# Keys, queries and rotary queries: high weights against both halves of the latent in one 512-column product

## The chip, the cores and the metric

The kernel runs on one core of a Trainium2 chip. The metric is the device time of one execution, in microseconds; beside it stands the span of one profiled execution, from its first to its last instruction. Lower is better.

## The reference

One layer of an encoder over 256 tokens of width 2048, with a last RMSNorm. All arrays are float32. Only the latent attention is touched here:

```python
def mla_branch(q_lat, kv_lat, k_rope, cos, sin, q_norm_w, w_uq, kv_norm_w, w_ukv, w_o_attn):
    q = (rms_norm(q_lat, q_norm_w) @ w_uq).reshape(bsz, s_len, MLA_HEADS, QK_NOPE_DIM + QK_ROPE_DIM)
    q_nope, q_rope = q[..., :QK_NOPE_DIM], q[..., QK_NOPE_DIM:]
    q_rope = apply_rope(q_rope, cos[:, :, None, :], sin[:, :, None, :])
    kv = (rms_norm(kv_lat, kv_norm_w) @ w_ukv).reshape(bsz, s_len, MLA_HEADS, QK_NOPE_DIM + V_HEAD_DIM)
    k_nope, v = kv[..., :QK_NOPE_DIM], kv[..., QK_NOPE_DIM:]
    ...
        sc = (jnp.einsum("bqhd,bkhd->bhqk", qn, k_nope)
              + jnp.einsum("bqhr,bkr->bhqk", qr, k_rope))
        p = jax.nn.softmax(sc.astype(jnp.float32) * scale, axis=-1).astype(v.dtype)
        return jnp.einsum("bhqk,bkhd->bqhd", p, v)
```

Both latents have 512 channels; there are 16 heads of 128 plain and 64 rotary channels. Around it the layer has a combined input projection, a two-way SSD scan, an output projection and a gated feed-forward part, which make up most of the time.

## The kernel before, in words

Every large product is done in float32r, a format that TensorE takes at one pass, with each operand split in a high part and a low part: high x high, high x low and low x high are summed, low x low is dropped. Weights come as blocks of 128 x 128. A **job** is up to 16 blocks of weights that SyncE loads into one `raw` buffer (three of them); a job has two **halves** of eight blocks. For each half ScalarE (ACT) casts the high part (`wh`, line 151), and VectorE (DVE) subtracts it from the raw weights to get the low part (`wl`, line 152). There are five buffers each of `wh` and `wl` (`HB=5`), so the split runs up to five halves ahead of TensorE (PE).

Activations are held channels first, 128 channels x 256 tokens. The large projections (`dense`, lines 178 and 185) keep high and low activations side by side, so that one product of 512 columns multiplies a high weight block with both; a bank of PSUM then holds two sums of 256 columns, and the low weights add 256 columns to the first. `halves_sum` (lines 237 and 238) adds the two sums: an ACT copy of one, a DVE add of the other. Gate units (`quad`, lines 213 to 215) and `v_job` (lines 573 to 575) have the activations as the stationary operand, and hold two banks.

The latent attention uses another form, `mm3` (lines 157 to 159): three products of 256 columns for each block, high weight x high latent, high weight x low latent, low weight x high latent, all into one sum. `lat_norm2` (lines 424 and 425) splits a latent into `latH` and `latL`. `qk_job` i has in its first half the queries of two heads, and in its second their keys; a half is two blocks of 128 channels x four blocks of 128 latent channels, and its two results lie side by side in one bank `g`. ACT casts it to the high part of `qk` (line 596), DVE subtracts to get the low part (line 597). `r_job` does the rotary queries of eight heads in the same way, with one ACT copy of the bank (line 537), after which four DMAs on ACT's queue fetch the swapped halves (line 377).

PSUM has eight banks: four for `g` and four for `s`, the attention's own small products. In the attention stage the jobs stand as written in a list, where g is a unit of a gate quad (four units in a row fill the same two banks), R the rotary queries, V the values and QK queries with keys:

```python
"g R0 g g g V0 QK0 g QK1 V1 QK2 g QK3 V2 R1 g QK4 g QK5 V3 QK6 g QK7 g g g g g"
```

The attention of a head (`att1`, scores and exponentials; `att2`, transposes of the probabilities; `att3`, the product with the values) is hung onto the jobs that follow. A scheduler then orders each engine's instructions and hands out buffers and banks as they come free, so the order on an engine is not that of the lines. ACT and DVE work in that order, one instruction after the other, and so does PE.

Of the kernel before, what the change touches and what calls it, by code (L numbers as in the profile page):

```python
# [15 lines left out]
P = 128  # L16
S = 256
# [42 lines left out]
def tile_bidir_hybrid_layer(ctx: ExitStack, tc, xT, pos, vec, cst, w_in, w_r, w_v, w_qk, w_oa,  # L60
# [23 lines left out]
    def f32(ap):  # L84
        return ap.bitcast(F32)
# [330 lines left out]
    def lat_norm2(which, wname):  # L416
        ps = spread(lat[which + "v"])
        r = p1(name="r_" + which)
        act.activation(r, ps, AF.Copy)
        t = lat[which]  # L420
        for k in range(4):
            dve.scalar_tensor_tensor(t[:, k, :], t[:, k, :], vcol(wname, k), r, ALU.mult, ALU.mult)
        hi, lo = page([P, 4, S], F32R, name="latH"), page([P, 4, S], F32R, name="latL")
        act.activation(hi, t, AF.Copy)
        dve.tensor_sub(lo, t, f32(hi))
        lat[which + "HL"] = (hi, lo)


    dts = {}
# [93 lines left out]
            dve.tensor_sub(z[r], t[r, 0, :], f32(kr["h"][r]))  # L523

    def r_job(i):
        hi, lo = lat["qHL"]
        cell = {}

        def mm(h, n, wh, wl):
            ps = gpsum([P, 2, S])  # L530
            cell[h] = ps
            for b in range(2):
                for k in range(4):
                    mm3(ps[:, b, :], wh[:, 4 * b + k, :], wl[:, 4 * b + k, :], hi[:, k, :], lo[:, k, :],
                        k == 0, k == 3)
            t = page([P, 2, S], name="rf")
            act.activation(t, ps, AF.Copy)
            cell["f", h] = (t, swapped(t, 2))

        def ev():  # L540
            pass

        def ro():
            for h in range(2):
                q, sw = cell["f", h]
                rotate(q, sw, 2)


                t = page([P, 2, 2, S], F32R, name="rp")
                for j in range(2):  # L550
                    s0, s1 = slice(64 * j, 64 * j + 64), slice(64 - 64 * j, 128 - 64 * j)
                    act.activation(t[s0, j], q[s0], AF.Copy)
                    dve.tensor_sub(t[s1, j], q[s0], f32(t[s0, j]))
                rp[2 * i + h] = t
        j = Job(w_r[i], 16, mm, ev)
        jobs.append(j)
        return j, ro

    def v_job(i):
        hi, lo = lat["kvHL"]  # L560
        cell = {}

        def mm(h, n, wh, wl):
# [4 lines left out]
            for t in range(2):  # L568
                ts = slice(t * P, (t + 1) * P)
                for kk in range(2):  # L570
                    k = 2 * h + kk
                    ps = cell["ps"][t]
                    pe.matmul(ps, lhsT=hi[:, k, ts], rhs=wH[:, kk, :], start=k == 0, stop=False)
                    pe.matmul(ps, lhsT=hi[:, k, ts], rhs=wL[:, kk, :], start=False, stop=False)
                    pe.matmul(ps, lhsT=lo[:, k, ts], rhs=wH[:, kk, :], start=False, stop=k == 3)

        def ev():
            vh, vl = page([P, 2, 512], F32R, name="vh"), page([P, 2, 512], F32R, name="vl")
# [7 lines left out]

    def qk_job(i):
        def mm(h, n, wh, wl):
            hi, lo = lat["qHL" if h == 0 else "kvHL"]
            ps = gpsum([P, 2, S])  # L590
            for b in range(2):
                for k in range(4):
                    mm3(ps[:, b, :], wh[:, 4 * b + k, :], wl[:, 4 * b + k, :], hi[:, k, :], lo[:, k, :],
                        k == 0, k == 3)
            t = page([P, 2, 2, S], F32R, name="qk")
            act.activation(t[:, 0], ps, AF.Copy)
            dve.tensor_sub(t[:, 1], ps, f32(t[:, 0]))
            qk[i, h] = t
        j = Job(w_qk[i], 16, mm, lambda: None)
        jobs.append(j)  # L600
        return j
# [700 lines left out]
```

## Time and profile before

| | before |
|---|---|
| time, median of 3 runs | 1962.59 us (1961.36 to 1962.71) |
| profiled execution | 1962.68 us |
| its span | 1960.9 us |
| mean granted clock of TensorE | 0.998 |
| attention stage (first R job's products to last QK job's) | about 75 to 235 us |
| HBM read | 371.91 MB |

PE is the row of the matmuls, PEld that of the weight loads that lie under them. A matmul's row is longer than the distance to the next one's start, since matmuls are pipelined; so prices are taken from starts. A line can be that of a helper: `mm3`'s lines 157 to 159 serve other stages too, told apart by the tile names (`latH`, `latL`).

### The profile page before, as it was taken

The page shows a single profiled execution, that of the slowest core. Times are in us where ns is not written, and L with a number is a line of the kernel's source. Part 1 is how long each engine was busy: PE and PEld are TensorE (multiplying, and loading weights), DVE is VectorE, ACT ScalarE, POOL GpSimd, SP SyncE. Part 2 cuts the span into 40 slices and gives each one's busy share as a digit, 9 for nine tenths or more (in the row PEclk, how much of TensorE's full clock was granted, in tenths as well). Part 3 has the DMA queues.
Part 4 walks back from the last instruction along what each step waited for, and adds up shares of the span by engine and source line. Part 5 has one row for each costly group of instructions (what it writes and reads, how often), then busy time and mean ns, then how long its engine had stood idle before and what let it go on. Part 6 is the DMA issues. An engine that isn't in the chain of part 4 may idle for free.

```text
span 1960.9 us, 28920 instructions
## 1 busy us (share of the span) xinstructions
PE 1945.8 (99%) x11136; PEld 1707.2 (87%) x11136; DVE 1444.6 (74%) x2349; ACT 1205.3 (61%) x1878; POOL 0.2 (0%) x4
## 2 busy tenths in 40 slices
PE   9999999999999999999999999999999999999997
PEld 8889988888888888888888888888888888888887
DVE  7897744779779789879755566777656777557775
ACT  6566544687887887978644455666435655346553
POOL 0000000000000000000000000000000000000000
PEclk9999999999999999999999999999999999999999
DMA  7554456765665565565666665555555555555543
GB/s 279 179 173 154 137 172 216 251 222 172 215 233 173 198 234 194 194 215 182 205 196 198 200 222 176 190 193 192 181 189 190 194 192 175 194 192 193 188 161 124
DMA packets 93259, 379.31 MB, mean 193 GB/s; under 512 B 10688, under 2 KB 11328, under 8 KB 62912
## 3 DMA queue, kind: packets, MB, share of 16 engines
q1 hardware_dynamic: 91440, 375.09, 56.6%
q10 hardware_dynamic: 1680, 2.37, 0.4%
q8 instruction: 87, 1.43, 0.3%
q14 instruction: 52, 0.43, 0.1%
HBM read 371.91 MB, written 4.33 MB: 192 GB/s over the span
## 4 chain that ended last, share of the span: by engine, by line
PE 95%; DVE 3%; DMA 1%; ACT 1%; issue 0%; ACTq 0%; DVEq 0%; SPq 0%
PE g L178 42%; PE g L185 22%; PE g L214 7%; PE g L213 7%; PE g L215 7%; PE g L159 1%; PE g L157 1%; PE g L158 1%; DVE wl L152 1%; PE s L789 1%; PE s L798 1%; PE s L158 0%; PE s L159 0%; PE s L157 0%; PE s L771 0%; PE s L634 0%
## 5 line engine op out<-in xcount | busy, mean ns | idle before, releaser
L152 DVE TENSOR_TENSOR wl<-raw,wh 128x1024 fp32r<-128x1024 f32 (+1 forms) x670 | 802.7, 1209 | 328.1 <-ACT wh L151 181.3
L151 ACT ACTIVATE wh<-raw 128x1024 fp32r<-128x1024 f32 (+1 forms) x670 | 698.9, 1047 | 546.6 <-PE g L178 352.0
L178 PE MATMUL g<-xHL,wh 128*128 128x512 f32 x1424 | 341.7, 392 | 1.3 <-DVE xHL L291 1.1
L178 PE MATMUL g<-hHL,wh 128*128 128x512 f32 x1360 | 324.8, 391 | 0.0
L178 PEld LDWEIGHTS g<-xHL,wh 128*128 128x128 f32 x1424 | 262.4, 188 | 53.6 <-DVE xHL L291 1.5
L178 PEld LDWEIGHTS g<-hHL,wh 128*128 128x128 f32 x1360 | 249.8, 188 | 48.3
L185 PEld LDWEIGHTS g<-xHL,wl 128*128 128x128 f32 x1424 | 182.6, 191 | 7.0
L185 PE MATMUL g<-xHL,wl 128*128 128x256 f32 x1424 | 184.9, 283 | 0.0
L185 PEld LDWEIGHTS g<-hHL,wl 128*128 128x128 f32 x1360 | 174.3, 191 | 6.6
L185 PE MATMUL g<-hHL,wl 128*128 128x256 f32 x1360 | 176.4, 283 | 0.0
L178 PE MATMUL g<-aHL,wh 128*128 128x512 f32 x692 | 166.6, 391 | 0.1
L910 DVE SCALAR_TENSOR_TENSOR uc<-u,V,uc 128x255 f32<-128x255 f32 x176 | 85.3, 485 | 88.4 <-ACT uc L908 85.3
L178 PEld LDWEIGHTS g<-aHL,wh 128*128 128x128 f32 x692 | 126.9, 188 | 25.6 <-DVE aHL L928 1.3
L213 PE MATMUL g<-wh,yHL 128*128 128x512 f32 x256 | 100.1, 391 | 0.0
L214 PE MATMUL g<-wl,xHL 128*128 128x512 f32 x256 | 100.0, 391 | 0.0
L213 PE MATMUL g<-wh,xHL 128*128 128x512 f32 x256 | 100.0, 391 | 0.0
L215 PE MATMUL g<-wh,yHL 128*128 128x512 f32 x256 | 99.7, 389 | 0.0
L215 PE MATMUL g<-wh,xHL 128*128 128x512 f32 x256 | 99.6, 389 | 0.0
L214 PE MATMUL g<-wl,yHL 128*128 128x512 f32 x256 | 99.6, 389 | 0.0
L185 PEld LDWEIGHTS g<-aHL,wl 128*128 128x128 f32 x692 | 89.2, 191 | 3.6
L185 PE MATMUL g<-aHL,wl 128*128 128x256 f32 x692 | 90.4, 283 | 0.0
L684 DVE SCALAR_TENSOR_TENSOR xs<-cu,V,xs 128x254 f32<-128x254 f32 (+1 forms) x128 | 59.0, 479 | 0.2
(298 smaller groups left out, 2534.1 us busy)
## 6 DMA issues: line engine op xcount, KB each, us to landing
raw<-in_w_in SPq DMA_DIRECT2D x88, 1024.0 KB, 4.9
raw<-in_w_up SPq DMA_DIRECT2D x88, 1024.0 KB, 4.8
raw<-in_w_in SPq DMA_DIRECT2D x128, 256.0 KB, 3.9
raw<-in_w_os SPq DMA_DIRECT2D x128, 256.0 KB, 3.6
raw<-in_w_dn SPq DMA_DIRECT2D x32, 1024.0 KB, 5.0
raw<-in_w_oa SPq DMA_DIRECT2D x64, 256.0 KB, 3.9
FB<-acsD SPq DMA_DIRECT2D x32, 512.0 KB, 7.4
raw<-in_w_out SPq DMA_DIRECT2D x14, 1024.0 KB, 5.0
```

The costliest lines, as they stand in the source:

```text
L151: act.activation(vh, r, AF.Copy)
L152: dve.tensor_sub(vl, r, f32(vh))
L157: pe.matmul(ps, lhsT=wH, rhs=xH, start=first, stop=False)
L158: pe.matmul(ps, lhsT=wH, rhs=xL, start=False, stop=False)
L159: pe.matmul(ps, lhsT=wL, rhs=xH, start=False, stop=last)
L178: pe.matmul(ps, lhsT=wh[:, b, :], rhs=x, start=k == 0, stop=False)
L185: pe.matmul(cell["ps"][:, 0, :], lhsT=wl[:, b, :], rhs=get(k)[:, 0, :], start=False, stop=k == ktot - 1)
L213: pe.matmul(ps, lhsT=x[:, 0, ts], rhs=wH[:, kk, :], start=k == 0, stop=False)
L214: pe.matmul(ps, lhsT=x[:, 0, ts], rhs=wL[:, kk, :], start=False, stop=False)
L215: pe.matmul(ps, lhsT=x[:, 1, ts], rhs=wH[:, kk, :], start=False, stop=k == kt - 1)
L684: dve.scalar_tensor_tensor(o[:, a], u[:, b], vcol("cw", k * 48 + cb), o[:, a], ALU.mult, ALU.add)
L910: dve.scalar_tensor_tensor(o[:, a], u[:, b], vcol("fcw", k * 88 + cb), o[:, a], ALU.mult, ALU.add)
```

## The change

`lat_norm2` now lays high and low latent side by side (`latHL`, in two tiles of two channel blocks), and `two_blocks` replaces `mm3` in `r_job` and `qk_job`. A half takes two banks, one for each block of output channels: eight products of 512 columns with the high weights, four per bank; then eight of 256 columns with the low weights; then `halves_sum` on each bank into a page of SBUF (`qkf`, or `rf` itself). For `qk_job` the cast and the subtraction follow, now from that page and no longer from PSUM. `v_job` only reads the latents from the new tiles.

```diff
--- before.py
+++ after.py
@@ -420,10 +420,28 @@
         t = lat[which]
         for k in range(4):
             dve.scalar_tensor_tensor(t[:, k, :], t[:, k, :], vcol(wname, k), r, ALU.mult, ALU.mult)
-        hi, lo = page([P, 4, S], F32R, name="latH"), page([P, 4, S], F32R, name="latL")
-        act.activation(hi, t, AF.Copy)
-        dve.tensor_sub(lo, t, f32(hi))
-        lat[which + "HL"] = (hi, lo)
+        for b in range(2):
+            v = page([P, 2, 2, S], F32R, name="latHL")
+            act.activation(v[:, 0], t[:, 2 * b:2 * b + 2, :], AF.Copy)
+            dve.tensor_sub(v[:, 1], t[:, 2 * b:2 * b + 2, :], f32(v[:, 0]))
+            lat[which + "HL", b] = v
+
+    def latk(which, k):
+
+        return lat[which + "HL", k // 2][:, :, k % 2, :]
+
+    def two_blocks(which, wh, wl, o):
+
+        ps = [gpsum([P, 2, S]), gpsum([P, 2, S])]
+        for b in range(2):
+            for k in range(4):
+                pe.matmul(ps[b], lhsT=wh[:, 4 * b + k, :], rhs=latk(which, k), start=k == 0, stop=False)
+        for b in range(2):
+            for k in range(4):
+                pe.matmul(ps[b][:, 0, :], lhsT=wl[:, 4 * b + k, :], rhs=latk(which, k)[:, 0, :], start=False,
+                          stop=k == 3)
+        for b in range(2):
+            halves_sum(ps[b], o[:, b, :])
 
 
     dts = {}
@@ -523,18 +541,11 @@
             dve.tensor_sub(z[r], t[r, 0, :], f32(kr["h"][r]))
 
     def r_job(i):
-        hi, lo = lat["qHL"]
         cell = {}
 
         def mm(h, n, wh, wl):
-            ps = gpsum([P, 2, S])
-            cell[h] = ps
-            for b in range(2):
-                for k in range(4):
-                    mm3(ps[:, b, :], wh[:, 4 * b + k, :], wl[:, 4 * b + k, :], hi[:, k, :], lo[:, k, :],
-                        k == 0, k == 3)
             t = page([P, 2, S], name="rf")
-            act.activation(t, ps, AF.Copy)
+            two_blocks("q", wh, wl, t)
             cell["f", h] = (t, swapped(t, 2))
 
         def ev():
@@ -557,7 +568,6 @@
         return j, ro
 
     def v_job(i):
-        hi, lo = lat["kvHL"]
         cell = {}
 
         def mm(h, n, wh, wl):
@@ -569,10 +579,11 @@
                 ts = slice(t * P, (t + 1) * P)
                 for kk in range(2):
                     k = 2 * h + kk
+                    x = latk("kv", k)
                     ps = cell["ps"][t]
-                    pe.matmul(ps, lhsT=hi[:, k, ts], rhs=wH[:, kk, :], start=k == 0, stop=False)
-                    pe.matmul(ps, lhsT=hi[:, k, ts], rhs=wL[:, kk, :], start=False, stop=False)
-                    pe.matmul(ps, lhsT=lo[:, k, ts], rhs=wH[:, kk, :], start=False, stop=k == 3)
+                    pe.matmul(ps, lhsT=x[:, 0, ts], rhs=wH[:, kk, :], start=k == 0, stop=False)
+                    pe.matmul(ps, lhsT=x[:, 0, ts], rhs=wL[:, kk, :], start=False, stop=False)
+                    pe.matmul(ps, lhsT=x[:, 1, ts], rhs=wH[:, kk, :], start=False, stop=k == 3)
 
         def ev():
             vh, vl = page([P, 2, 512], F32R, name="vh"), page([P, 2, 512], F32R, name="vl")
@@ -586,15 +597,11 @@
 
     def qk_job(i):
         def mm(h, n, wh, wl):
-            hi, lo = lat["qHL" if h == 0 else "kvHL"]
-            ps = gpsum([P, 2, S])
-            for b in range(2):
-                for k in range(4):
-                    mm3(ps[:, b, :], wh[:, 4 * b + k, :], wl[:, 4 * b + k, :], hi[:, k, :], lo[:, k, :],
-                        k == 0, k == 3)
+            o = page([P, 2, S], name="qkf")
+            two_blocks("q" if h == 0 else "kv", wh, wl, o)
             t = page([P, 2, 2, S], F32R, name="qk")
-            act.activation(t[:, 0], ps, AF.Copy)
-            dve.tensor_sub(t[:, 1], ps, f32(t[:, 0]))
+            act.activation(t[:, 0], o, AF.Copy)
+            dve.tensor_sub(t[:, 1], o, f32(t[:, 0]))
             qk[i, h] = t
         j = Job(w_qk[i], 16, mm, lambda: None)
         jobs.append(j)
```

The scheduler's order changes on PE, DVE and ACT in the attention stage; SyncE's order stays. Of three places the rows follow, with what each first instruction waits for where it does. Tiles have a number each: `g_` is a tile of one PSUM bank.

First PE around QK0. Before, this is the end of QK0's second half (`g_1132`), and the gate unit behind it, whose banks `g_1166` and `g_1167` are those of V0:

```order
L159 MATMUL g_1132<-latH_949,wl_1031 128x256
L157 MATMUL g_1132<-latH_949,wh_1030 128x256
L158 MATMUL g_1132<-latL_950,wh_1030 128x256
L159 MATMUL g_1132<-latH_949,wl_1031 128x256
L213 MATMUL g_1166<-wh_1054,xHL_491 128x512 [waits DVE_49]
L214 MATMUL g_1166<-wl_1055,xHL_491 128x512
L215 MATMUL g_1166<-wh_1054,xHL_491 128x512
L213 MATMUL g_1167<-wh_1054,xHL_491 128x512 [waits DVE_49]
```

In the change, the end of QK0's first half (`g_1097`, `g_1098`) and the begin of its second (`g_1127`, `g_1128`):

```order
L441 MATMUL g_1097<-latHL_705,wl_1011 128x256 [waits DVE_49]
L441 MATMUL g_1097<-latHL_705,wl_1011 128x256
L441 MATMUL g_1097<-latHL_708,wl_1011 128x256 x2
L441 MATMUL g_1098<-latHL_705,wl_1011 128x256 x2
L441 MATMUL g_1098<-latHL_708,wl_1011 128x256 x2
L438 MATMUL g_1127<-latHL_943,wh_1026 128x512 [waits DVE_49]
L438 MATMUL g_1127<-latHL_943,wh_1026 128x512
L438 MATMUL g_1127<-latHL_946,wh_1026 128x512 x2
L438 MATMUL g_1128<-latHL_943,wh_1026 128x512 [waits DVE_49]
```

The wait for DVE, which was before the gate unit, now stands before QK0's second half: with two banks for each half this half takes the banks of V0, and the gate unit behind it those of QK0's first half.

Second, DVE at QK1, between the two halves' evacuations. Before (`qk_1247` is the result of the first half, `wl_1251` low weights of a later half, `o` and `t` belong to a softplus, `sm` and `p` to the attention):

```order
L624 RECIPROCAL sm_1209<-sm_1209 128x2 [waits Activation_49]
L456 TENSOR_TENSOR o_2945<-o_2945,t2_2944 128x256 [waits DVE_49]
L626 TENSOR_SCALAR p_1212<-p_1212,sm_1209 128x256 [waits DVE_49]
L626 TENSOR_SCALAR p_1212<-p_1212,sm_1209 128x256
L597 TENSOR_TENSOR qk_1247<-g_1222,qk_1247 128x512 [waits Activation_49]
L152 TENSOR_TENSOR wl_1251<-raw_1196,wh_1250 128x1024 [waits Activation_49]
L457 TENSOR_SCALAR o_2945<-o_2945 128x256 [waits DVE_49]
L456 TENSOR_TENSOR o_2945<-o_2945,t2_2944 128x256 [waits DVE_49]
```

In the change (`wl_1241` are the same later low weights, `g_1215` and `g_1216` the first half's banks, `qkf_1214` their page):

```order
L152 TENSOR_TENSOR wl_1211<-raw_1188,wh_1210 128x1024 [waits DMAHW1_49,Activation_49]
L626 TENSOR_SCALAR sm_1201<-sm_1201 128x2 [waits DVE_49]
L469 TENSOR_TENSOR t_2899<-t_2899,e_2898 128x256
L470 TENSOR_TENSOR t2_2900<-t_2899 128x256 [waits DVE_49]
L152 TENSOR_TENSOR wl_1241<-raw_1188,wh_1240 128x1024 [waits PE_49,Activation_49]
L631 RECIPROCAL sm_1201<-sm_1201 128x2 [waits Activation_49]
L238 TENSOR_TENSOR qkf_1214<-qkf_1214,g_1215 128x256 [waits Activation_49]
L633 TENSOR_SCALAR p_1204<-p_1204,sm_1201 128x256 [waits DVE_49]
L633 TENSOR_SCALAR p_1204<-p_1204,sm_1201 128x256
L238 TENSOR_TENSOR qkf_1214<-qkf_1214,g_1216 128x256 [waits Activation_49]
```

The low-weight subtraction, which came behind the first half's evacuation, is now ahead of it, and it waits for PE, whose first half reads the buffer that it writes; PE's second half waits for the two adds of line 238.

Third, PE at QK4 and QK5. Before, QK4's second half (`g_1974`, one bank) is followed by an attention product (`s_2004`):

```order
L157 MATMUL g_1974<-latH_949,wh_1792 128x256
L158 MATMUL g_1974<-latL_950,wh_1792 128x256
L159 MATMUL g_1974<-latH_949,wl_1793 128x256
L157 MATMUL s_2004<-pT_1919,vh_1349 128x256 [waits Activation_49]
L158 MATMUL s_2004<-pT_1919,vh_1349 128x256 [waits DVE_49]
L159 MATMUL s_2004<-pT_1919,vl_1350 128x256
L157 MATMUL s_2004<-pT_1919,vh_1349 128x256
L158 MATMUL s_2004<-pT_1919,vh_1349 128x256
L159 MATMUL s_2004<-pT_1919,vl_1350 128x256
L213 MATMUL g_1166<-wh_1870,xHL_632 128x512
```

In the change, QK4's second half (`g_1945`, `g_1946`) is followed by QK5's first (`g_2043`, `g_2044`):

```order
L438 MATMUL g_1946<-latHL_946,wh_1768 128x512 x2
L441 MATMUL g_1945<-latHL_943,wl_1769 128x256 x2
L441 MATMUL g_1945<-latHL_946,wl_1769 128x256 x2
L441 MATMUL g_1946<-latHL_943,wl_1769 128x256 x2
L441 MATMUL g_1946<-latHL_946,wl_1769 128x256 x2
L438 MATMUL g_2043<-latHL_705,wh_1910 128x512 [waits DVE_49]
L438 MATMUL g_2043<-latHL_705,wh_1910 128x512
L438 MATMUL g_2043<-latHL_708,wh_1910 128x512 x2
L438 MATMUL g_2044<-latHL_705,wh_1910 128x512 [waits DVE_49]
L157 MATMUL s_2018<-qk_1967,qk_1937 128x256 [waits Activation_49]
```

QK4's second half now stands behind the gate unit and waits for the adds of QK4's first half, and QK5's first half comes directly behind it and waits for its adds, on the same two banks.

## The prediction

> **What bounds the kernel now.** I read the page's span, busy times and chain first.
>
> ```profile
> span 1960.9 us, 28920 instructions
> ...
> PE 1945.8 (99%) x11136; PEld 1707.2 (87%) x11136; DVE 1444.6 (74%) x2349; ACT 1205.3 (61%) x1878; POOL 0.2 (0%) x4
> ...
> PE 95%; DVE 3%; DMA 1%; ACT 1%; issue 0%; ACTq 0%; DVEq 0%; SPq 0%
> ```
>
> PE is busy 99% of the span and is 95% of the chain that ended last. So a matmul that costs less ends the kernel earlier, and a microsecond in which PE stands still ends it later. The change touches only the attention stage, about 75 to 235 us, so the second view is the busy time by stretches there (columns: PE, PEld, DVE, ACT, POOL, clock, DMA share, GB/s), and the third is who PE waits for between 60 and 260 us.
>
> ```profile
> 100.00:110.00 10.00, 8.62 (x56) 7.42 (x54) 9.80 (x14) 8.70 (x13) 0.00 (x0) 1.00 0.50 168
> 110.00:120.00 10.00, 10.00 (x64) 9.04 (x63) 9.71 (x13) 3.81 (x5) 0.00 (x0) 1.00 0.90 321
> 150.00:160.00 10.00, 10.00 (x75) 9.54 (x74) 7.22 (x14) 4.95 (x11) 0.00 (x0) 1.00 0.46 158
> ...
> PE g L159 <- DVE wl L152: 1.1, 1, 1.1
> PE g L574 <- DVE wl L152: 0.3, 1, 0.3
> ```
>
> Two regimes: around 100 to 120 us DVE is full (9.8 and 9.7 of 10) and PE waits for it twice, 1.4 us in all; by 150 us DVE has over a quarter of its time free and PE waits for nobody. The granted clock is 1.00 throughout.
>
> **The matmuls.** Next are the groups of the three lines of `mm3`, on the high and low latents, and the cadence of matmuls. A row's duration holds the pipeline's fill, so the price is the distance of two starts: first starts of two neighbouring halves of 24 products, then a run of 13 products of 512 columns, one of 16 of 256, and what follows.
>
> ```profile
> L157 PE MATMUL g<-latH,wh x160: 277/283/364, 75.2 to 229.5; 128*128 128x256 f32 x160
> L158 PE MATMUL g<-latL,wh x160: 278/283/283, 76.6 to 229.6; 128*128 128x256 f32 x160
> L159 PE MATMUL g<-latH,wl x160: 278/283/384, 76.7 to 229.7; 128*128 128x256 f32 x160
> L157 PEld LDWEIGHTS g<-latH,wh x160: 187/192/192, 75.0 to 229.4; 128*128 128x128 f32 x160
> ...
> 133.24 0.28 PE L157 MATMUL g<-latH,wh 128*128 128x256 f32 x1
> 136.12 0.28 PE L157 MATMUL g<-latH,wh 128*128 128x256 f32 x1
> ...
> 1211.81 3.12 PE L178 MATMUL g<-hHL,wh 128*128 128x512 f32 x13
> 1214.76 2.08 PE L185 MATMUL g<-hHL,wl 128*128 128x256 f32 x16
> 1216.68 0.50 PE L252 MATMUL s<-ones,ssh 128*128 128x1 f32 x4
> ```
>
> A half takes (136.12 - 133.24) = 2.88 us for 24 products, 0.120 each. A 512-column product takes (1214.76 - 1211.81)/13 = 0.227, a 256-column one (1216.68 - 1214.76)/16 = 0.120. A half becomes 8 x 0.227 + 8 x 0.120 = 2.78 us. The columns streamed are the same; only 8 starts of some 0.013 us go. There are 480/24 = 20 halves (4 of `w_r`, 16 of `w_qk`): **-20 x 0.10 = -1.9 us** (-1.8 with 0.229, which longer runs average). That is 0.1% of the span at best.
>
> The Trainium skill (TensorE: Matmul & The Clock Gate, "Back-to-back issue gap") puts a warm product at N/2.4 + 2.5 ns apart from the next. By it 3 x 109.2 ns become 215.8 + 109.2, an estimated 0.4 us over 160 pairs; the starts above are 0.120 and 0.227 apart, not 0.109 and 0.216, and the trace decides.
>
> **The evacuations.** Before, a half is one bank, read by ACT and DVE at 512 columns. Now it is two banks, each read by an ACT copy and a DVE add of 256 columns, and then cast and subtracted from SBUF at 512.
>
> ```profile
> L596 ACT ACTIVATE qk<-g x16: 580/584/600, 109.5 to 230.9; 128x512 fp32r<-128x512 f32 x16
> L597 DVE TENSOR_TENSOR qk<-g,qk x16: 681/684/691, 111.3 to 232.2; 128x512 fp32r<-128x512 f32 x16
> L237 ACT ACTIVATE u<-g x85: 376/384/386, 1220.5 to 1875.7; 128x256 f32<-128x256 f32 x85
> L238 DVE TENSOR_TENSOR u<-u,g x85: 411/414/420, 1220.9 to 1876.8; 128x256 f32<-128x256 f32 x85
> ...
> 115.12 1.23 DVE L152 TENSOR_TENSOR wl<-raw,wh 128x1024 fp32r<-128x1024 f32 x1 [0.26 <-ACT wh L151]
> 128.39 0.40 PE L574 MATMUL g<-wl,latH 128*128 128x512 f32 x1
> ```
>
> So DVE gains 40 adds of 0.41, 16.6 us, and ACT some 0.77 a half of w_qk, about 12 us, less for w_r. After 150 us DVE's idle quarter takes this. Between 110 and 140 us some six halves add 5 us to a DVE without a gap; but the low weights made at 115.12 to 116.35 are first read by V1's product at 128.39, 12 us later, which covers it. Splitting a latent into two pieces of 512 columns costs only two starts. Queues and DMA issues keep their order. These I set at nothing; with that cover gone it would be up to 5 us.
>
> **The banks** are what I charge for. The pool of `g` has four. A gate unit or `v_job` holds two, so a half that needs two leaves no spare: the next half can start only when this one's adds are done. Four places follow, in order of time.
>
> ```profile
> 89.96 0.69 DVE L382 TENSOR_TENSOR sw<-sw,sinT 128x512 f32<-128x512 f32 x1 [2.43 <-DMA sw<-rf]
> 95.83 1.22 DVE L152 TENSOR_TENSOR wl<-raw,wh 128x1024 fp32r<-128x1024 f32 x1
> 104.43 4.63 DVE L152 TENSOR_TENSOR wl<-raw,wh 128x1024 fp32r<-128x1024 f32 x4
> 108.98 1.28 DVE L581 TENSOR_TENSOR vl<-g,vh 128x512 fp32r<-128x512 f32 x2
> ...
> 111.08 0.40 PE L213 MATMUL g<-wh,xHL 128*128 128x512 f32 x1
> ```
>
> *V0 to QK0.* QK0's second half now needs V0's two banks, which the gate unit behind it needed before; they are wanted one half earlier. They come free with the `vl` subtractions, first at 108.98 + 0.60 = 109.6, behind a DVE that has not paused since 89.96. In the new order that chain has the rope key's add (0.43) in it: 110.0. Its first low weights were ready at 95.83 + 1.22 = 97.05; the new order has the latent's second piece (0.6), the rotary split (1.4) and that add ahead of them, some 2.8 us with the starts, 99.9. Behind them V0 has 22 of its 24 products, 22 x 0.229 = 5.0, to 105, and QK0's first half 2.8, to 107.8; PE waits 2.2 us, ends the second half at 112.8 and starts the gate unit then, not at 111.08: **+1.8**. Between -0.5 (DVE early) and +3.8 (the rotary half's DMAs, now issued behind an add, land 2 us later).
>
> *QK1, first to second half.* The order puts a low-weight subtraction (1.23 in the row of 115.12) between the first half's products and its first add, and has it wait for PE: it writes the buffer this half reads. So after the half's last product come 0.16 of pipeline (0.28 less 0.12), 1.23, and an add of 0.41, with starts 1.9 us: **+1.9** (0.6, the bare copy and add less the second bank's 0.48, to 2.5).
>
> ```profile
> 181.48 0.68 DVE L637 TENSOR_TENSOR pT<-s,pT 128x512 fp32r<-128x512 f32 x1
> 182.19 1.39 DVE L553 TENSOR_TENSOR rp<-rf,rp 64x512 fp32r<-64x512 f32 x2
> ...
> 188.97 1.29 DVE L597 TENSOR_TENSOR qk<-g,qk 128x512 fp32r<-128x512 f32 x2
> ```
>
> *QK4, first to second half.* DVE still runs the same list between splitting a `pT` (done 182.1) and QK4's first evacuation (188.97): 6.9 us, plus an add, 7.3. Before, nobody waited for it. Now PE, after the attention product that needs this `pT`, has 5 products of 0.12 and 17 of 0.227, 4.5 us, before QK4's second half wants the banks. It gets there 6 x 0.120 + 7 x 0.227 + 0.12 = 2.4 us after its transposes, while a copy and a subtraction of 512 columns (0.58 and 0.68 above) with 0.2 of starts take 1.5: some 1 us after `pT` is done. So 7.3 - 1.0 - 4.5: **+1.7**, rounded down for a PE that is late by other waits (0 to 2.8).
>
> *QK4 to QK5.* QK5 follows directly on the same two banks. On ACT a high-weight cast (1.06 by the row below) waits for the half's last high product at 1.9 of 2.78 us, the copy stands behind it, then the add: 1.9 + 1.06 + 0.38 + 0.41 + 0.1 = 3.9, less 2.78: **+1.1** (0.6 to 2).
>
> ```profile
> 185.66 1.06 ACT L151 ACTIVATE wh<-raw 128x1024 fp32r<-128x1024 f32 x1 [1.82 <-PE g L158]
> ```
>
> At QK2, QK3, QK7 and the two R jobs the order has 0.7 to 2.3 us of other products in between; I give them **+0.4** together (0 to 1.5).
>
> The Trainium skill (Perfetto Trace Analysis, "Optimization Strategy") says that the same gap repeating on the engine that should be full can mean too little PSUM for the next tile. By it the four places cost what is summed below; without it the sum would be the bare -1.9 us. This trace, where a half takes one bank, shows no such gap.
>
> **Sum.** -1.9 + 1.8 + 1.9 + 1.7 + 1.1 + 0.4 = **+5.0 us**. The profiled execution took 1962.7 us (span 1960.9 and 1.8 around it), as good as the median of the three runs, 1962.59: **1967.6 us**. I call 0.2%, 3.9 us, what a measurement of this kernel can tell from no change; the forecast is just beyond it. Bounds: -1.9 - 0.5 + 0.6 + 0 + 0.6 + 0 = -1.2 and -1.9 + 3.8 + 2.5 + 2.8 + 2.0 + 1.5 = +10.7.
>
> **The rivals.**
> *The waits are small or covered* (0.35). If ACT and DVE are punctual, the two middle places vanish and the first shrinks to nothing: -1.9 + 0 + 0.6 + 0 + 0.6 = -0.7, 1962 us; with half of my waits, -1.9 + 3.5 = +1.6, 1964 us. Not slower. It decides when adds come within about 0.6 us of the end of a half. For it: DVE is free for a quarter of its time after 150 us. Against it: queues are in order, and the low-weight casts stand ahead of the adds.
> *The gain stands and old waits go too* (0.05). QK0 begins with 8 high products, and so needs its low weights 1.8 us later; the 1.4 us of waits at 100 to 106 us go with no new one: -1.9 - 1.4 = -3.3 us, 1959.4, at the edge of 0.2%: I put 0.03 of it beyond. Against it: DVE, not the place of the low products, sets that stretch.
> *Weight loads cost time of their own* (0.02). 160 loads go; at 0.19 by their row that is 30 us, 1932. The loads' rows are longer than the 0.120 between starts, so they lie under the products and save nothing.
> The Trainium skill (TensorE: Matmul & The Clock Gate, "The mechanism") says loads overlap products only when their row groups differ, and these are all full-height; with its 107 ns a load, an estimate of 17 us saved. The trace disagrees, as above.
> *DVE becomes the bound of the stage* (0.08). If the 16.6 us on DVE delay the low weights too, up to 5 us on top of the sum, 1973 us or more. Against it: the low weights' lead.
>
> The forecast itself has 0.50. All cases follow from the order of a scheduler, not of the lines; the change does what it says in that order, 320 products for 480.
>
> **Range.** 1960.5 to 1973.5 us: from somewhat under the punctual case to the sum's upper bound; it leaves out most of two small rivals and the ends. Slower by over 0.2% (above 1966.5): 0.47 of the forecast's 0.50, the rest of it falling short, and the DVE rival's 0.08, 0.55. Within 0.2%: 0.35 + 0.03 + 0.02 = 0.40. Faster (below 1958.7): 0.03 + 0.02 = 0.05.
>
> **What would show it.** In the changed profile: 160 products of 512 columns 0.227 apart and 160 of 256 columns; PE waiting for DVE adds (line 238) and `vl` subtractions before the first product of a half, some 2 us each near 110, 125, and once or twice near 190 us, and no such wait where other products lie between; gate unit of QK1 starting near 113; the rest of the span as long as before. It is wrong if PE waits less than 2 us for adds and `vl` in all, if low weights are waited for past 115 us, or if stages behind 260 us change length.

## The result, and the profile after

| | before | after |
|---|---|---|
| time, median | 1962.65 us (4 runs, 1961.36 to 1962.71) | 1972.83 us (4 runs, 1971.71 to 1975.59) |
| ratio | | 1.0055, 95% interval 1.0039 to 1.0071 |
| profiled execution, its span | 1962.68 us, 1960.9 us | 1972.14 us, 1970.3 us |

The change makes the kernel 10.2 us slower, 0.55%. The page of the changed kernel:

```profile
span 1970.3 us, 28677 instructions
...
PE 1947.0 (99%) x10976; PEld 1700.3 (86%) x10976; DVE 1457.6 (74%) x2391; ACT 1215.3 (62%) x1916; POOL 0.2 (0%) x4
...
PE 94%; DVE 3%; ACT 1%; DMA 1%; issue 0%; ACTq 0%; SPq 0%; DVEq 0%
```

The 160 products are gone (11136 to 10976), and with them 160 weight loads. PE's busy time has not shrunk: it is 1947.0, where it was 1945.8. DVE has 13 us more work and ACT 10. PE idles more: 1970.3 - 1947.0 = 23.3 us, where it was 15.1. The whole difference lies in the attention stage: the first product on the attention's output (line 213 on `oT`) starts at 275.40 us, and started at 266.12 before, 9.3 of the 9.4 us between the spans.

PE's busy time holds what is lost at half clock (stretches in which the granted clock of TensorE is 0.50), of which more below.

Next, who PE waits for between 95 and 215 us (microseconds in all, times, longest), then the products of `two_blocks` and the starts of two neighbouring halves of QK6:

```profile
PE g L438 <- DVE qkf L238: 5.9, 4, 1.9
PE g L438 <- DVE vl L592: 1.9, 1, 1.9
PE g L585 <- DVE wl L152: 0.8, 1, 0.8
PE s L641 <- DVE p L633: 0.4, 1, 0.4
```

```profile
L438 PE MATMUL g<-latHL,wh x160: 387/393/632, 75.3 to 239.2; 128*128 128x512 f32 x160
L441 PE MATMUL g<-latHL,wl x160: 274/283/419, 77.1 to 240.3; 128*128 128x256 f32 x160
...
217.54 2.00 PE L438 MATMUL g<-latHL,wh 128*128 128x512 f32 x8
219.38 1.12 PE L441 MATMUL g<-latHL,wl 128*128 128x256 f32 x8
220.33 2.00 PE L438 MATMUL g<-latHL,wh 128*128 128x512 f32 x8
```

A half takes 220.33 - 217.54 = 2.79 us for 2.88, so the products save 20 x 0.09 = 1.8 us, as far as PE does not stand still. But it stands still 9.0 us in this stage, where it was 1.4. 7.8 us of it come ahead of high products (line 438), and what ends these waits are the sums (`qkf`, line 238) and the subtraction of V0's low parts (`vl`). Both read a bank of PSUM that the next half is to write, so these are waits for a bank. The maxima of the durations, 632 and 419 ns beside medians of 393 and 283, say something else: some products ran at half the clock.

```profile
109.00:113.00 4.00, 3.81 (x15) 3.31 (x16) 3.66 (x6) 1.12 (x2) 0.00 (x0) 0.69 0.98 393
```

In the row of 109 to 113 us (PE, PEld, DVE, ACT, POOL, clock, DMA share, GB/s) the granted clock is 0.69 on average. It was 1.00 in each row of this stage before.

How a bank comes back late is best seen at QK1, from its first to its second half (a row has start, duration, engine and line; in brackets the engine's idle time before it, and what ended it):

```profile
122.41 1.06 ACT L151 ACTIVATE wh<-raw 128x1024 fp32r<-128x1024 f32 x1 [2.03 <-PE g L438]
...
123.50 1.23 DVE L152 TENSOR_TENSOR wl<-raw,wh 128x1024 fp32r<-128x1024 f32 x1
...
124.28 0.65 ACT L237 ACTIVATE qkf<-g 128x256 f32<-128x256 f32 x2
...
124.72 0.40 DVE L238 TENSOR_TENSOR qkf<-qkf,g 128x256 f32<-128x256 f32 x1
...
125.18 1.19 PE L438 MATMUL g<-latHL,wh 128*128 128x512 f32 x4 [1.91 <-DVE qkf L238]
```

ACT has stood still for 2.03 us before 122.41, until this half's last high product freed a `wh` buffer. Then it casts the next high weights (1.06), computes two exponentials (to 124.28), and only then makes the copy that the first sum needs. DVE is held until 124.73 by the low weights that follow from the same cast. So two queues deliver at the same moment, 124.7, and the first add ends at 125.12; PE starts at 125.18.

### The profile page after: what moved, and what is told of

Read it like the earlier page. It is cut to its first block, busy times and chain, and to the rows that moved or that the text cites. A ratio compares the mean times of both kernels' runs of the same rounds, so it can differ in the third digit from the quotient of the medians.

```text
span 1970.3 us, 28677 instructions
## 1 busy us (share of the span) xinstructions
PE 1947.0 (99%) x10976; PEld 1700.3 (86%) x10976; DVE 1457.6 (74%) x2391; ACT 1215.3 (62%) x1916; POOL 0.2 (0%) x4
## 4 chain that ended last, share of the span: by engine, by line
PE 94%; DVE 3%; ACT 1%; DMA 1%; issue 0%; ACTq 0%; SPq 0%; DVEq 0%
PE g L178 42%; PE g L185 22%; PE g L214 7%; PE g L213 7%; PE g L215 7%; PE g L438 2%; DVE wl L152 1%; PE s L796 1%; PE g L441 1%; PE s L805 1%; PE g L159 0%; PE g L158 0%; PE g L157 0%; PE s L157 0%; PE s L159 0%; PE s L158 0%
```

## The experiments

Times are medians; "over before" is against the kernel before on the same chip (1962.23 to 1962.33 us). Beside each time stands the span of its profile and what that execution lost in stretches at half clock. The loss is worked out from the starts: within such a stretch products of 256 columns start 0.214 us apart, where they usually start 0.120 us apart, so that 3.4 us, the length of every one of these stretches, lose about 1.5.

| kernel | time, us | ratio, 95% interval | over before | span | lost at half clock |
|---|---|---|---|---|---|
| changed kernel again | 1972.74 | 1.0050 (1.0037 to 1.0063) | +10.4 | 1968.8 | 0 |
| two banks, old products, no sums | 1971.88 | 1.0047 (1.0033 to 1.0061) | +9.5 | 1970.2 | 2.9 |
| one bank, old products, sums | 1967.83 | 1.0030 (1.0018 to 1.0041) | +5.5 | 1965.9 | 0 |
| two banks, old products, sums | 1973.01 | 1.0054 (1.0040 to 1.0068) | +10.7 | 1972.8 | 4.5 |
| block by block | 1970.62 | 1.0042 (1.0030 to 1.0055) | +8.3 | 1968.8 | 1.5 |
| r_jobs undone | 1970.04 | 1.0039 (1.0026 to 1.0052) | +7.8 | 1966.3 | 0 |
| five banks for g | 1967.18 | 1.0028 (1.0017 to 1.0039) | +4.9 | 1965.2 | 1.5 |
| before, five banks for g | 1962.67 | 1.0003 (0.9994 to 1.0012) | +0.4 | 1961.5 | 0 |
| sums first | 1970.36 | 1.0043 (1.0029 to 1.0057) | +8.1 | 1968.6 | 0 |
| block by block, five banks | 1965.26 | 1.0015 (1.0006 to 1.0024) | +3.0 | 1963.9 | 0 |
| the same, sums first | 1967.54 | 1.0027 (1.0016 to 1.0038) | +5.3 | 1966.8 | 1.5 |

The theory: a half that holds two banks leaves no spare one, so that the next waits for its evacuation (banks). The rival: the waits come from the evacuation's own work on ACT and DVE, whatever the banks (work).

### Banks without work, work without banks

Two kernels with the products of before, each with one half of the suspicion. The first, from the kernel before:

```diff
-            ps = gpsum([P, 2, S])
+            ps = [gpsum([P, S]), gpsum([P, S])]
             for b in range(2):
                 for k in range(4):
-                    mm3(ps[:, b, :], ...)
+                    pe.matmul(ps[b], lhsT=wh[:, 4 * b + k, :], rhs=hi[:, k, :], start=k == 0, stop=False)
+                    pe.matmul(ps[b], lhsT=wh[:, 4 * b + k, :], rhs=lo[:, k, :], start=False, stop=False)
+            for b in range(2):
+                for k in range(4):
+                    pe.matmul(ps[b], lhsT=wl[:, 4 * b + k, :], rhs=hi[:, k, :], start=False, stop=k == 3)
...
-            act.activation(t[:, 0], ps, AF.Copy)
-            dve.tensor_sub(t[:, 1], ps, f32(t[:, 0]))
+            for b in range(2):
+                act.activation(t[:, 0, b, :], ps[b], AF.Copy)
+                dve.tensor_sub(t[:, 1, b, :], ps[b], f32(t[:, 0, b, :]))
```

> The kernel before, with its 480 products of 256 columns, but each half takes two banks of g, one for each block of output channels, with the low-weight products of both blocks last, and each bank is evacuated by its own ACT and DVE instruction of 256 columns straight from PSUM (no sum of halves, no qkf). It has the banks of the change without its products and without its sums. Banks theory (a half that holds two banks makes the next one wait for its evacuation): PE waits for that evacuation at the five places where the changed kernel shows 2.0, 2.1, 1.2, 2.1 and 1.1 us, 8.5 us in all, and nothing is saved on products: +7 to +11 us, 1970 to 1974 us. Rival, work theory (not the banks but the 16.6 us of adds on DVE and 12 us of copies on ACT make everything late): the extra work here is 0.14 us a half on DVE, 3 us in all and mostly covered: -1 to +2 us, 1962 to 1965 us.

It took 1971.88 us, +9.5: within the banks theory's range, with almost no work added. But the waits are fewer than the 8.5 us at five places that it expected. For evacuations by DVE PE waits 5.1 us at three places (the longer `qk` wait is QK1's):

```profile
PE g L433 <- DVE qk L601: 2.9, 2, 1.9
PE g L433 <- DVE vl L588: 2.2, 1, 2.2
```

Two stretches at half clock add 2.9 us; without them the span would be 1967.3 us, 6.4 over that of the kernel before. Its QK1 has the chain of the changed kernel: on ACT the cast at 121.94 us, two exponentials, the evacuation at 123.80, and then

```profile
124.32 0.40 DVE L601 TENSOR_TENSOR qk<-g,qk 128x256 fp32r<-128x256 f32 x1
...
124.78 0.39 PE L433 MATMUL g<-latH,wh 128*128 128x256 f32 x1 [1.92 <-DVE qk L601]
```

1.92 us of wait for 1.91, without a sum of halves. One thing it shares with the change beside the banks: all high products of a half come first, so their weight buffer is free before the half ends, and the order has the cast into it ahead of the evacuation. In the kernel before, this half was evacuated at 121.09 us, and the cast came after it. So the two banks are what PE waits for, and the order is part of why they come late. No run has the high products first in a single bank, so what this order costs by itself is not shown.

The second has one bank for a half, and copies and adds per block:

```diff
+    def zero_sum(ps, o):
+        for b in range(2):
+            act.activation(o[:, b, :], ps[:, b, :], AF.Copy, scale=0.0)
+            dve.tensor_add(o[:, b, :], o[:, b, :], ps[:, b, :])
...
-            act.activation(t[:, 0], ps, AF.Copy)
-            dve.tensor_sub(t[:, 1], ps, f32(t[:, 0]))
+            o = page([P, 2, S], name="qkf")
+            zero_sum(ps, o)
+            act.activation(t[:, 0], o, AF.Copy)
+            dve.tensor_sub(t[:, 1], o, f32(t[:, 0]))
```

> The kernel before, with its products and its one bank for a half, but evacuated by as many instructions as in the changed kernel: per block an ACT copy of 256 columns (scaled by zero) and a DVE add of 256 columns from the bank, then cast and subtraction from SBUF. It has the evacuation work of the change without its banks and its products. Banks theory: the spare banks cover later adds, -1 to +3 us, 1962 to 1966 us. Work theory: the waits are those of the changed kernel and no product is saved, +8 to +12 us, 1971 to 1975 us.

It took 1967.83 us, +5.5: above the banks theory's range (up to +3), below the work theory's (from +8). Neither of the two is right alone. So the work is not free. PE's waits between 95 and 210 us:

```profile
PE g L157 <- ACT gate L667: 1.6, 1, 1.6
PE g L157 <- DVE qkf L432: 1.3, 2, 0.9
PE g L213 <- ACT wh L151: 1.1, 1, 1.1
PE g L214 <- DVE wl L152: 0.7, 1, 0.7
```

The first two are bank waits too: the gate's evacuation at 104 us and adds at 195 and 198 us now come so late that a spare bank no longer covers them. In the others PE lacks weights (`wh`, `wl`), 1.8 us near 125 us. So the cover that the prediction named for the extra work was thinner than it said.

Both together, still with the old products (the first kernel with the copies and adds of the second on its two banks):

> The kernel before with both at once: its 480 products of 256 columns, two banks for a half, and the ACT copy and DVE add of each block. So it is the changed kernel in all but the products. Banks alone cost +9.5 us and the evacuation work alone +5.5 us, the changed kernel +10.4. Theory of one bound (PE waits for the time at which a bank comes back; a bank too few asks for it sooner, the work gives it back later, and at one place only the later of two reasons counts): less than the sum 15.0 by several us, and above the changed kernel by what the products are worth, 1.4 to 1.9 us: +11 to +13 us, 1973.5 to 1975.5 us. Rival, two separate costs that add: +14 to +16 us, 1976.5 to 1978.5 us. Rival, the merged products are worth nothing because PE waits anyway: +9.5 to +11 us, the changed kernel's time.

1973.01 us, +10.7, not the 15.0 of two costs that add. That fits the theory of one bound: a bank is missed sooner with one and comes back later with the other, and of two reasons at one place only the later counts. But it is also not above the changed kernel, as that theory had it, but level with it, as the last rival said: the 1.8 us that the merged products save do not show in the time. This profile has the most half clock of all; without it its span would be 1972.8 - 4.5 = 1968.3, and that of the changed kernel, run again without any, was 1968.8. A PE that is earlier waits longer at the next late bank: the waits for banks are 7.0 us here, 7.8 in the changed kernel.

### The changed kernel again, and the clock

> The changed kernel as it is, once more on the chip of the others, for its time beside theirs and for the half clock at 110.6 to 114 us of its profile. Both theories: +8 to +12 us, 1971 to 1975 us, with waits of PE for line 238 and vl of 8 us. If the half clock follows from the idle 2 us ahead of it, the profile shows a stretch at half clock again behind one of the idle stretches of about 2 us; if it depends on more than that, it is absent or behind another one, and the time is 1.6 us less.

1972.74 us, between 1970.68 and 1973.46. The profiled execution has the same waits (5.9 and 1.9 us, the longest 1.9) and no half clock in this stage; its span is 1.5 us under that of the first, which had one stretch. Here is the same window as above in this run:

```profile
109.00:113.00 4.00, 4.00 (x22) 3.44 (x23) 3.72 (x6) 1.94 (x4) 0.00 (x0) 1.00 0.91 377
```

The last kernel above had three stretches, in these windows:

```profile
109.00:113.00 4.00, 3.62 (x18) 3.62 (x19) 3.85 (x6) 0.00 (x0) 0.00 (x0) 0.57 1.01 424
125.00:129.50 4.50, 4.08 (x22) 4.08 (x23) 3.59 (x11) 1.76 (x3) 0.00 (x0) 0.65 0.68 233
197.50:202.00 4.50, 4.38 (x24) 4.38 (x24) 3.60 (x6) 1.65 (x3) 0.00 (x0) 0.62 0.60 200
```

What a stretch costs is seen on eight products of 256 columns, first in the changed kernel's stretch, then in this run:

```profile
111.63 1.91 PE L441 MATMUL g<-latHL,wl 128*128 128x256 f32 x8
110.86 1.12 PE L441 MATMUL g<-latHL,wl 128*128 128x256 f32 x8
```

The same order of instructions has the stretch in one execution (0.69) and not in another (1.00). In the profiles of the changed kernel and of the experiments, 20 idle times of PE in this stage were 1.8 us or longer. A stretch at half clock began at the end of 10 of them, from 0.2 us before it to 1.6 us after it, and no stretch of this stage began elsewhere. So here no stretch came without such a stall, and half of the stalls had none.

### One part undone: two blocks in a run

```diff
         for b in range(2):
+            ps = gpsum([P, 2, S])
             for k in range(4):
-                pe.matmul(ps[b], lhsT=wh[:, 4 * b + k, :], ...)
-        for b in range(2):
+                pe.matmul(ps, lhsT=wh[:, 4 * b + k, :], ...)
             for k in range(4):
-                pe.matmul(ps[b][:, 0, :], lhsT=wl[:, 4 * b + k, :], ...)
-        for b in range(2):
-            halves_sum(ps[b], o[:, b, :])
+                pe.matmul(ps[:, 0, :], lhsT=wl[:, 4 * b + k, :], ...)
+            halves_sum(ps, o[:, b, :])
```

> The changed kernel with one of its parts undone: the two blocks are no longer in one run. The first block has its four high and four low products, then its sum; then the second block. Products, instructions on ACT and DVE and banks are as many, but the first bank is done 1.4 us earlier (4 x 0.227 + 4 x 0.120), and the next half needs the second bank 1.4 us later. Banks theory: each wait shrinks by up to 1.4 us, so of 8.5 us at five places some 2 us are left: +0 to +4 us over the kernel before, 1962 to 1966 us. Work theory: the same work, so the same time as the changed kernel, +8 to +12 us, 1971 to 1975 us.

1970.62 us, +8.3: the expectation of the banks theory failed, and QK1 shows where.

```profile
122.96 1.06 ACT L151 ACTIVATE wh<-raw 128x1024 fp32r<-128x1024 f32 x1 [2.52 <-PE g L438]
...
124.82 0.65 ACT L237 ACTIVATE qkf<-g 128x256 f32<-128x256 f32 x2
...
125.82 1.17 PE L438 MATMUL g<-latHL,wh 128*128 128x512 f32 x4 [2.48 <-DVE qkf L238]
```

The first block's bank is complete 1.4 us earlier, but nothing evacuates it then. The copy stands behind the high-weight cast, and that waits for the last high product of the half, which in this form is even later (ACT idles 2.52 us before it). The bank is given back by ACT's queue, not by the products. The two waits that vanished are those of QK3 and QK5. The same kernel, still with four banks, in one more execution:

> The changed kernel block by block, as it was run before, once more for one look on this chip: both theories +7 to +9.5 us, 1969.5 to 1972 us; what differs between profiles of the same order is then the half clock alone (0, 1.4 or 2.8 us).

It gave 1969.8 us with the same waits to 0.1 us and its half clock at another place, from 124.2 us behind QK1's stall and no longer from 110.8.

### One part undone: the r_jobs

```diff
-            two_blocks("q", wh, wl, t)
+            act.activation(t, one_bank("q", wh, wl), AF.Copy)
```

> The changed kernel with the two r_jobs as before: mm3 into one bank, one ACT copy of 512 columns, no adds. Theory: the rotary halves' adds delay the rotary chain (swap DMAs, line 382 to 384, rp), which stands on DVE ahead of QK4's adds and of V0's vl; without them the wait in front of QK4's second half (2.1 us) and QK0's (2.0 us) shrink by 0.5 to 1.5 us each, the others (QK1, QK3, QK5) stay, and four halves lose 0.1 us each: +7 to +9.5 us, 1969 to 1972 us. Rival, only banks count: no r_job half was waited for, so nothing gets better and four halves cost 0.1 us each more: +10.5 to +11 us, 1973 us.

1970.04 us, +7.8, within the expectation. With four of twenty halves undone, 2.6 us come back, though PE had never waited for one of these four. Ahead of QK4's second half PE now loses 1.4 us instead of 2.1, ahead of QK0's 1.9 instead of 2.0, and the wait for low weights at 98 us, 0.7, is gone. The span is 2.5 us under that of the changed kernel run again, neither with half clock; 0.6 of it lies behind the attention stage. So the rotary halves delay what stands behind them. This run takes both their adds and their second banks away, so it does not tell which of the two does it. For the adds speaks QK4: in the changed kernel the last of the rotary chain on DVE (`rp`) is followed without a pause by QK4's adds, and PE, free since 194.7, goes on at 196.63:

```profile
193.38 1.22 DVE L152 TENSOR_TENSOR wl<-raw,wh 128x1024 fp32r<-128x1024 f32 x1
194.63 1.40 DVE L564 TENSOR_TENSOR rp<-rf,rp 64x512 fp32r<-64x512 f32 x2
196.06 0.75 DVE L238 TENSOR_TENSOR qkf<-qkf,g 128x256 f32<-128x256 f32 x2
```

### A fifth bank

PSUM's eight banks are divided anew, in the changed kernel and in the one before:

```diff
-    gps = ctx.enter_context(tc.tile_pool(name="gps", bufs=4, space=bass.MemoryType.PSUM))
-    sps = ctx.enter_context(tc.tile_pool(name="sps", bufs=4, space=bass.MemoryType.PSUM))
+    gps = ctx.enter_context(tc.tile_pool(name="gps", bufs=5, space=bass.MemoryType.PSUM))
+    sps = ctx.enter_context(tc.tile_pool(name="sps", bufs=3, space=bass.MemoryType.PSUM))
```

> The changed kernel with five banks for g and three for s, one spare bank beside a gate unit's and a half's. Banks theory: the next half can run its first block's four high products, 0.9 us, before it needs a bank that is not yet evacuated, so each of five waits is 0.9 us shorter, 4 us in all; the loss of an s bank is priced by the kernel before with the same division, in the same run. Difference of the two: +5 to +7.5 us, where it is 10.4 with four banks. Work theory: the adds come as late with five banks as with four, and the low weights too: difference +9 to +11 us.

> The kernel before with five banks for g and three for s: the price of an s bank less, for the comparison above. Both theories: no half waits for its bank in the kernel before, so the fifth g bank saves nothing, except perhaps at the waits of 101 to 106 us; attention's own small products may wait for the third bank: 0 to +5 us, 1962 to 1967 us.

1967.18 and 1962.67 us: the difference is 4.5 us where it is 10.4 with four banks, a little more gain than the banks theory had claimed. The kernel before loses nothing that can be told by giving an `s` bank away. QK1 shows that this is the bank and not a better order:

```profile
119.32 1.06 ACT L151 ACTIVATE wh<-raw 128x1024 fp32r<-128x1024 f32 x1 [2.03 <-PE g L438]
121.78 0.65 ACT L237 ACTIVATE qkf<-g 128x256 f32<-128x256 f32 x2
...
119.06 1.12 PE L441 MATMUL g<-latHL,wl 128*128 128x256 f32 x8
120.01 1.09 PE L438 MATMUL g<-latHL,wh 128*128 128x512 f32 x4
```

On ACT the copy still stands behind the same cast and two exponentials, and comes 2.46 us after the cast's start (1.87 with four banks). But PE goes from the first half into the second without a pause at 120.01, since a bank is free. So the main cause is the missing bank: with the same instructions and one bank more, over half of the cost is gone. What stays with five banks, in the changed kernel:

```profile
PE g L438 <- DVE qkf L238: 1.9, 1, 1.9
PE s L641 <- DVE p L633: 1.6, 2, 1.1
PE g L438 <- DVE vl L592: 1.4, 1, 1.4
```

Of four waits for sums one is left, QK4's, which is as long as with four banks; the theory had each of five waits 0.9 us shorter. Part of QK1's comes back as a wait for `p` (1.1 us), which follows from the same exponentials. The Trainium skill (Perfetto Trace Analysis, "Optimization Strategy") reads the same gap repeating on the engine that should be full as possibly too little PSUM; the trace agrees, 7.8 us of such gaps with four banks and 3.3 with five.

### The sums first

Four banks again, and in the scheduler the sums before anything else that is ready:

```diff
+            with tc.high_priority():
-            halves_sum(ps[b], o[:, b, :])
+                halves_sum(ps[b], o[:, b, :])
```

> The changed kernel with the sums of halves at high priority for the scheduler, so that in ACT's and DVE's order a half's copies and adds stand ahead of casts, low-weight subtractions and the rotary chain that before stood between. Four banks, same instructions. Theory of order (a bank comes back late because its sum stands in a queue behind work that nobody waits for as urgently): the waits in front of the second halves of QK1, QK3 and QK4 and in front of QK5, 6.4 us in all, fall to the bare copy and add, some 0.6 to 1 us each; V0's vl (2.0 us) is not touched: +5.5 to +8 us, 1968 to 1970 us. Rival, DVE has no time there (9.5 to 9.9 of 10 us busy until 150 us), so what is put first only makes low weights late in its place: +9.5 to +12 us, 1972 to 1974 us, with PE waiting for line 152.

1970.36 us, +8.1, just above what the theory of order allowed (+8), and not in the way it said. QK4's wait is gone, those of QK1 (1.85), QK3 (1.07) and in front of QK5 (1.14) are not; at QK1 the copy still comes behind the cast that waits for PE. And the rival's sign is there, a new wait for low weights:

```profile
PE g L438 <- DVE qkf L238: 4.1, 3, 1.8
PE g L586 <- DVE wl L152: 2.5, 1, 2.5
```

Order moves the cost about; it takes little of it away.

### Block by block with five banks

The two edits above together, and then with the sums first as well:

> The changed kernel block by block and with five banks for g and three for s. The first block's bank is done 1.4 us before the half's end, and the next half asks for it only with its second block, another 1.4 us after its start, so its sum has 2.8 us where the changed kernel gives it none. Banks theory: waits that are under 2.8 us without it go altogether, and QK4's, behind the rotary chain, is 0 to 2 us: -1 to +3 us, 1961 to 1965 us, and at least 2 us under the 1967.2 us of five banks alone. Rival, five banks alone had taken all that banks can give and the rest is work on ACT and DVE: +4 to +6 us, 1966 to 1968 us.

> Block by block, five banks for g, three for s, and the sums of halves at high priority. If banks and order are the whole cost, nothing is left but the saving on products, 1.4 to 1.8 us, and V0's and the low weights' own waits: -2 to +1.5 us, 1960.5 to 1964 us. If the work on DVE is a bound of its own, the sums that go first push the low weights back, and PE waits for line 152: +2 to +6 us, 1964 to 1968 us.

The first took 1965.26 us, +3.0, at the upper end of the expectation, and 1.9 us under five banks alone where at least 2 were expected. For sums PE now waits only 0.2 us; its longest waits are others:

```profile
PE s L158 <- DVE pT L642: 1.6, 1, 1.6
PE s L639 <- DVE p L631: 1.3, 1, 1.3
PE g L438 <- DVE vl L590: 0.9, 1, 0.9
```

With the banks nearly out of the way PE waits for DVE's other results, `pT` and `p`, 2.9 us, more than the products can save. The second, with the sums first, is slower again, 1967.54 us, within what was expected if the work is a bound of its own: 2.2 us of waiting for `oT`, 2.6 for `wl`. I read this as the work's own price: once banks are there, the adds on DVE delay what stands behind them. No version beat the kernel before. The nearest with merged products is 0.15% behind it (0.06 to 0.24%).

## Why the prediction was right, and where its sizes were off

The forecast was slower, by +5.0 us; it is +10.2, twice as much and near the upper bound. The mechanism it charged for, banks that are asked for before the adds have freed them, is the main one: five banks take 10.4 down to 4.5. The two places that it named near 110 and 125 us and the two near 190 are four of the five waits for banks. Step by step:

- **The matmuls**, -1.9: 2.79 us a half for 2.88, -1.8. The size is right, but as the kernel with the old products shows, a PE that waits for banks gains nothing by being early.
- **V0 to QK0**, +1.8 (112.8 - 111.08 is rather 1.7): PE waited 1.88 us for `vl` (forecast 2.2). Its gate unit started at 113.34 us, 2.3 us late, but some 1.3 of that is half clock; run again without it, at 111.81, 0.7 late. PE began QK0's second half at 109.19, forecast for 110.0: `vl` came earlier than reckoned. The term is too high by a microsecond, and the half clock, of which it knew nothing, hides that in the total. That the gate unit started near 113, as the prediction had it, was luck.
- **QK1**, +1.9: 1.91 of idle PE. The size is right, the reason only in part. The low-weight subtraction does stand ahead of the add, but on ACT the cast and two exponentials stand ahead of the copy, too, and both queues deliver at 124.7. This is why neither earlier products nor sums first helped there.
- **QK4**, +1.7: 1.92 of idle PE, and on DVE the list that was reckoned: from the end of `pT` at 189.60 to the first add at 196.06. **QK4 to QK5**, +1.1: 0.93. Both are about as reckoned.
- **The others**, +0.4 (0 to 1.5): here the sum failed. QK3 alone costs 1.13 us of idle PE:

```profile
155.70 1.06 ACT L151 ACTIVATE wh<-raw 128x1024 fp32r<-128x1024 f32 x1 [2.21 <-PE g L438]
...
157.56 0.65 ACT L237 ACTIVATE qkf<-g 128x256 f32<-128x256 f32 x2
...
158.47 1.20 PE L438 MATMUL g<-latHL,wh 128*128 128x512 f32 x4 [1.13 <-DVE qkf L238]
```

  The prediction trusted in the 0.7 us of other products that the order has there. The cast that waits for the half's last high product was charged at QK5 only, and nowhere with the exponentials behind it. From the moment at which the last high product lets the cast go, 155.70, it takes 2.8 us of cast, two exponentials, copy and add until PE can go on at 158.47. `p` at 208 us adds 0.4, a wait of attention and not of a bank, and the 0.8 us for low weights at 98 us stand where before had 1.4 at 101 to 106.
- **What no term had**: the half clock, 1.5 us in this execution; and about a quarter of a microsecond beside each wait (only QK1's term has part of it). The pipeline empties (0.16, the matmul's row of 0.28 less its 0.12), and the first starts behind a wait are slower: four products take 1.19 us at 125.18, and 1.07 at 205.62, both at a granted clock of 1.00.

```profile
205.62 1.07 PE L438 MATMUL g<-latHL,wh 128*128 128x512 f32 x4
```

  Seven waits make it 7 x 0.28 = 2.0 us, an estimate from this pair of rows; before had two waits, 0.6.

Set beside the 9.4 us between the spans: -1.8 of products, +7.6 of idle PE (9.0 less 1.4), +1.5 of half clock, +1.4 beside five waits more make +8.7. The remaining 0.7 is not assigned.

Of the rivals, **DVE as the bound** named 1973 us, the time that was measured, but for another reason. DVE has 13.0 us more to do, where 16.6 were reckoned, and this is in the result as a share, not as the case: low weights are waited for only at 98 us, and the work without the banks costs 5.5 us, nearly the 5 us that the prediction named if the cover failed, but together with the banks it adds 1.2 to two_banks' 9.5. **Waits small or covered** fell with the four waits (its sum keeps 0.6 us at QK1, though its words let both middle places vanish). **Weight loads** of their own cost fell, since PE's busy time did not shrink. **The gain stands** fell too: a wait for low weights is still there, at 98 us, and new ones came.

What stays open: why the half clock follows one stall and not its twin, what having the high products first costs by itself, and how much of the 5.5 us of work is order and how much DVE's time. Every one of these kernels has a somewhat different order on ACT and DVE, and the runs cannot hold it fixed.

## What to carry to other kernels

A form that saves products but holds twice the PSUM has to be paid for by the slowest queue in front of its evacuation. Look at what stands ahead of that copy on ACT, above all an instruction that itself waits for the same run of products, before counting on early products or on priorities. Where PE is full and DVE nearly so, a saving of 0.1% in products is lost by the first late bank (1.8 us saved, 1.9 us lost at QK1 alone). Give the banks first (five instead of four cost the kernel before nothing that could be told here), then try the form; here even that left it 3.0 us behind at best.

## What the runs showed of the hardware

A stall of PE of about 2 us can cost more than itself: in 10 of 20 cases the granted clock fell to 0.50 for 3.4 us soon after it, about 1.5 us lost. The nine runs of the changed kernel lie between 1970.7 and 1975.6 us, the 14 runs of the kernel before beside them within 1.4 us; stretches at half clock that come and go would spread times so, though only the profiles show them. The Trainium skill (TensorE: Matmul & The Clock Gate, "HAM oscillation — how this bites in real kernels") warns of idle gaps above 3.4 us. Here gaps of 1.8 to 2.5 us were enough, and the measurement decides. That it varies from run to run fits what the same page says of a free-running window ("What's actually happening"); no run here shows the window itself.
